# Half of one gate ahead of the mixing projection, and the transposes of the first tiles one product step later

## The chip, the cores and the metric

The kernel runs on one core of one Trainium2 chip. The metric is the time of one execution on the device in microseconds (us): the median of several runs. One more execution was recorded by the hardware profiler, and the rows shown below are from it. The engines are called as in the profile: PE (TensorE, matrix products and transposes), PEld (its weight loads), DVE (VectorE), ACT (ScalarE), POOL (GpSimd) and SP (SyncE, which issues most of the loads). Each engine, and each DMA queue, works its instructions off in the order in which they were laid down.

## The reference

One layer of an encoder with d = 1024 and 1024 tokens, all in float32:

```
x = x + 1/2 * post1(SwiGLU_1(pre1(x)))          # FFN 1, inner width 2816
u = pre_mix(x)
ret_q, ret_k, ret_v, ret_g, na_q, na_k, na_v, gate_ret, gate_na = split(u @ W_mix_in)
y_ret = (silu(ret_g) * headnorm(retention in both directions)) @ W_ret_out
y_na  = (neighbourhood attention on a 16 x 64 grid, with bias) @ W_na_out
x = x + post_mix((sigmoid(gate_ret) * y_ret + sigmoid(gate_na) * y_na) @ W_mix_out)
x = x + 1/2 * post2(SwiGLU_2(pre2(x)))          # FFN 2
```

pre, post and headnorm are RMS norms. `gate_na` is a 1024 x 1024 array: eight blocks of 128 channels, each for two halves of 512 tokens. The change is about the first half of its block 4.

## The kernel before

Every float32 operand is split into two parts, h (a cast on ACT) and l (a subtraction on DVE, `split`, lines 60 and 61), and each product is the sum of three matmuls (`mm3`, lines 87 to 89): h with h, h with l, l with h. Weights come by `load_w`: a 512 KB load on SP's queue into one of three `wraw` buffers, then two pieces of 512 columns, each one cast on ACT and one subtraction on DVE (`wl`, line 61), in a ring of eight pieces. There are eight PSUM banks: six of tag `ps`, two of tag `pt`.

The large products use seven half-size products instead of eight (Winograd's form). Tokens are handled in eight tiles of 128, t0 to t7. For such a product the left operand needs, beside its quarters a11, a12 (tiles t0 to t3) and a22, four sums s1 to s4, which are made while the tiles t4 to t7 are put away (`Winograd.put`).

The stages in order, with their place in the profile: FFN 1 in; FFN 1 out (`ffn_out`, up to about 681 us); the last tiles of it (to about 738 us); the mixing projection (`Pairs.run` over `jobs`, to about 1030 us); neighbourhood attention (`na_cores`); retention (`ret_cores`, to about 1449 us); its output product and W_mix_out; FFN 2 in; FFN 2 out.

**FFN out.** `ffn_out` walks 77 steps, n = 11 i + k: seven products i, eleven steps k of 12 matmuls each. Products with even i use four `ps` banks, those with odd i use two `ps` and two `pt`. After the fifth product (i = 4) the rows of t0 to t3 are complete. What is left for each, the four stages of `stages`, is put in the list `later`, and one entry is taken off ahead of the matmuls of each of the following steps, from n = 55 on:

- stage 0: a sum of squares finished on DVE (line 488) and its power -1/2 on POOL (`rstd`, line 97)
- stage 1: two residual additions on DVE (line 493), two stores of x on SP's queue, two squares on ACT (line 496)
- stage 2: the second norm's sum (DVE, line 500), `rstd` on POOL, two scalings on DVE (line 504)
- stage 3: eight transposes on PE (`flip`, line 126) into `ps` banks while i = 5 and into `pt` banks after it, and `put`: casts on ACT, subtractions on DVE.

So t0 has the steps 55 to 58, t1 59 to 62, t2 63 to 66, t3 67 to 70. At the end of the sixth product (i = 5, n = 65) `p2` adds to the four banks (DVE, line 581), and a square on ACT (line 482) reads the result and uses the bank as its waste, the `pt` banks too. In FFN 2 out there is no second norm: `stages` has the first two entries only.

**Between FFN out and the mixing projection.** `ffn_out` returns four `flips`, those of t4 to t7. Each makes its first four transposes into a `pt` bank, whose put copies to ACT (line 272) and forms part of s3 on DVE (lines 276, 277), and its second four into another, whose put splits a22 and makes s1, s2 and s3 (DVE 282, 284 and three subtractions; POOL 287, 288 for s4). Between them PE is given other work by a `Filler`: a generator of steps of three matmuls, of which so many are taken as the tuple `FLIP_FILL` says:

```
    fill = Filler(first())
    for f, k in zip(rest, FLIP_FILL):
        fill(k)
        f = f()
        if f is not None:
            fill(FLIP_FILL[4])
            f()
```

`first()` gives 32 steps of `vproj` (na_v for t0 to t3; line 1120 copies its banks out) and 24 of `mx.leads()`, the first products of the three first jobs, which fill all six `ps` banks. What is left is drained, and then the first job's `run` copies its lead to SBUF (line 376) and starts on the product with s2.

**The attention stages.** `products()` is the second filler: 385 steps in all: ret_v (128 steps and a mark), the blocks 4 to 7 of `gate_na` (`gate`, 16 steps each, sigmoid on ACT, line 1210), `gate_ret`, and the product W_na_out (64 steps, multiplied with the gate on DVE, line 1243). `NA_FILL` takes 12 + 34 x 4 = 148 steps in neighbourhood attention and `RET_FILL` takes 14 + 4 x 54 + 4 = 234 in retention. The last three are drained behind it. The last retention chunks go through `norm` (lines 929 to 937, with `rstd` on POOL), transposes (line 946), and a multiplication (line 947) with a tile `rg` that is loaded on SP's queue into one of two buffers. The product W_ret_out then starts on `xy`, the split of what retention has stored.

The order on each engine is not the text's order alone: a planner puts the instructions of each engine in a list by its own estimates of when they are ready, with the text's order as priority. An instruction whose operands it holds to be ready may be placed before an earlier one.

Of the kernel before, what the change touches and what calls it, by code (L numbers as in the profile page):

```python
# [10 lines left out]
F32 = mybir.dt.float32  # L11
F32R = mybir.dt.float32r
AF = mybir.ActivationFunctionType
# [5 lines left out]
P = 128  # L19
D = 1024  # L20
S = 1024
KT = D // P
# [6 lines left out]

NA_FILL = (12, 2, 2)  # L30
RET_FILL = (14, 2, 2, 4, 2, 3, 0, 1, 2)
FLIP_FILL = (8, 8, 8, 8, 2)
NA_UNITS = ((0, 0, 0), (3, 1, 0), (1, 0, 1), (1, 0, 2), (4, 1, 1), (4, 1, 2), (2, 0, 3), (5, 1, 3))
KEY_OFF = (0, 8, 24, 32)
RET_SCALE = 128 ** -0.5
# [387 lines left out]
class LeftFactors:  # L423


    order = [j + h * FT // 2 for j in range(FT // 2) for h in range(2)]
# [108 lines left out]
def ffn_out(c, q, blocks, junk, xtile, w_out, t_out, gl, ep, side={}):  # L535


    nc = c.nc
    NK = FT // 2
    tt = nc.vector.tensor_tensor  # L540
    later, rest, flips, xs = [], [], [], {}

    def xload(t):

# [23 lines left out]
    def p4(u, b):  # L568
        tt(q[3][:, u], b, q[3][:, u], ALU.add)
        ep.square(u, 0, q[3][:, u], b)  # L570
        later.extend(stages(u, (q[3][:, u], q[2][:, u])))

    def stages(t, halves):
        g = ep.steps(t, xs[t], halves)

        f = []
        return [lambda: next(g), lambda: next(g)] + [
            lambda: f.append(next(g)), lambda: f[0](*(("ps", 6) if i < 6 else ("pt", 2)))] * (ep.pre is not None)
# [431 lines left out]
def trunk_layer(ctx: ExitStack, tc, x, g1a, w1i, w1o, g1b, gma, wmt, wnv, wrv, logits, dtab, rope, bias,  # L1010
                wro, wno, wmo, gmb, g2a, w2i, w2o, g2b, out):
    nc = tc.nc
# [5 lines left out]
    c = Core(tc, const, wpool, psum, dram)  # L1018
# [4 lines left out]
    def dt(name, shape):  # L1023
        return dram.tile(shape, F32, name=name)
# [4 lines left out]
    d = {  # L1029
        "a21": dt("a21", [P, 4, 512]),  # L1030
        "nq": dt("nq", [NHP, P, S]), "nk": dt("nk", [NHP, P, S]), "nv": dt("nv", [16, 64, 512]), "nvg": dt("nvg", [4, 4, P, 512]),
        "no": dt("no", [NHP, P, S]), "rq": dt("rq", [RH, P, S]), "rk": dt("rk", [RH, P, S]),
        "rv": dt("rv", [TT, P, D]), "rg": dt("rg", [8, P, S]), "ry": dt("ry", [8, P, S]),
        "sr": dt("sr", [8, P, S]), "sn": dt("sn", [8, P, S]), "z": dt("z", [8, P, S]), "m": dt("m", [8, P, S]),
    }
# [24 lines left out]
    with (tc.tile_pool(name="tw1", bufs=1, reuse_waits="tile") as tw,  # L1060
# [12 lines left out]
    q = [ep.tile([P, 4, 512], F32, tag="q", name="q", bufs=2) for _ in range(2)]  # L1073
# [9 lines left out]
    rest = ffn_out(c, q, Blocks(c, (g0, g0, g0, g1), (3, 1)), junk,  # L1083
                   lambda t: (m1, m2, ep, ep)[t // 2].tile([P, D], F32, tag="xs", name="xs", bufs=2 + t // 4 * 2),
                   w1o, t1o, gl[0], fo,
                   {n: (lambda j=j: ahead.update({j: c.load_w(wnv[j])})) for j, n in enumerate((65, 66))})
# [8 lines left out]
    def xh(t, k):  # L1095

        return a21 if (t, k) == (1, 0) else wx.op(("a11", "a12", None, "a22")[2 * t + k])

    def vproj(src, groups, done):

        for toks in groups:
            banks = {t: c.bank() for t in toks}
            for k in range(KT):
                if k % 2 == 0:
                    w = ahead.pop(k // 2) if k // 2 in ahead else c.load_w(src[k // 2])
                for t in toks:
                    tt = slice((t % 4) * P, (t % 4 + 1) * P)
                    c.mm3(banks[t], [q[:, k % 4, tt] for q in xh(t // 4, k // 4)], w[k % 2], k == 0, k == KT - 1)
                    yield
            for t in toks:  # L1110
                done(t, banks[t])

    evpool = []

    def ev():
        return evpool[0].tile([P, S], F32, tag="ev", name="ev", bufs=3)
# [18 lines left out]
    jobs += [(32 + 2 * i, 33 + 2 * i, d["sn"][2 * i], d["sn"][2 * i + 1], AF.Sigmoid) for i in range(2)]  # L1135
    mx = Pairs(c, wx, [(wmt[j[0]], wmt[j[1]]) for j in jobs], 3)

    def first():
        yield from vproj(wnv, ((0, 1, 2, 3),), done_nv)
        yield from mx.leads()  # L1140

    fill = Filler(first())
    evpool[:] = [wx.tmp, None]
# [6 lines that stand above are left out]
    g_stack.close()  # L1150
    ep_stack.close()
    with tc.tile_pool(name="pa", bufs=1, reuse_waits="tile") as pa:
# [12 lines left out]
        for i, (_, _, f, g, fn) in enumerate(jobs):  # L1165
# [6 lines left out]
            def done(j):  # L1172
                h = j % 2
                if fn == "rotary":
                    rotate(turners[j], half(), parts[j], *tabs[h])
                elif fn is not None:
                    nc.scalar.activation(parts[j], parts[j], fn)
                c.store((f, g)[j // 2][:, h * 512:(h + 1) * 512], parts[j])
# [17 lines left out]
    mix.tile([P, 40], F32, name="pad")  # L1196
    evpool[:] = [mix]

    def gate(i, dst, halves=(0, 1)):

        w = c.load_w(wmt[i])
        e = ev()
        for h in halves:
            hs = slice(h * 512, (h + 1) * 512)
            b = c.bank()
            for k in range(KT):
                ks = slice((k % 4) * P, (k % 4 + 1) * P)
                c.mm3(b, [p[:, ks] for p in w[k // 4]], [q[:, k % 4] for q in xh(h, k // 4)], k == 0, k == KT - 1)
                yield
            nc.scalar.activation(e[:, hs], b, AF.Sigmoid)  # L1210
        hs = slice(halves[0] * 512, halves[-1] * 512 + 512)
        c.store(dst[:, hs], e[:, hs])

    def products():
        for j in range(2):
            yield from vproj(wrv[j], ((0, 1, 2), (3, 4, 5), (6, 7)), done_rv(j))
        yield "rv"
        for i in range(4, 8):
            yield from gate(32 + i, d["sn"][i])
        for i in range(4):  # L1220
            yield from gate(24 + i, d["sr"][i])
        for i in range(4, 8):
            yield from gate(24 + i, d["sr"][i], (1,))
        x1_stack.close()
        opool = pool(o_stack, "o", "right")
        oop = [opool.tile([P, 4, S], F32R, name=f"o{q}") for q in "hl"]
        for i in range(4, 8):
            raw = c.raw(d["no"][i - 4])
            c.split(oop[0][:, i - 4], oop[1][:, i - 4], raw)
            yield from gate(24 + i, d["sr"][i], (0,))  # L1230

        for i in range(8):
            if i % 2 == 0:
                w = c.load_w(wno[i // 2])
            e = ev()
            nc.sync.dma_start(e, d["sn"][i])
            for h in range(2):
                hs = slice(h * 512, (h + 1) * 512)
                b = c.bank()
                for k in range(4):  # L1240
                    c.mm3(b, [p[:, k * P:(k + 1) * P] for p in w[i % 2]], [q[:, k, hs] for q in oop], k == 0, k == 3)
                    yield
                nc.vector.tensor_tensor(e[:, hs], b, e[:, hs], ALU.mult)
            c.store(d["z"][i], e)
# [23 lines left out]
    for i0 in (0, 3, 6):  # L1268
        tiles = range(i0, min(i0 + 3, 8))
        m, z, w, banks = {}, {}, {}, {}  # L1270
# [16 lines left out]
        for i in tiles:  # L1287
            for k in range(KT if i0 > 0 else 0):
                one(i, k)
            for h in range(2):  # L1290
                hs = slice(h * 512, (h + 1) * 512)
# [11 lines left out]
    with tc.tile_pool(name="ep2", bufs=1, reuse_waits="tile") as ep:  # L1303
        rest = c.out_proj(KT, stream(c, gs, lambda k: d["m"][k]), lambda k: c.load_w(wmo[k]),
                          Ep(c, ep, gmb, g2a, False, rows(x1), rows(x2), wx.put))
# [19 lines left out]
    q = [op.tile([P, 4, 512], F32, tag="q", name="q", bufs=4) for _ in range(4)]  # L1325
# [86 lines left out]
```

## Time and profile before

| | before |
|---|---|
| median of 3 runs | 2304.51 us (2303.83 to 2305.05) |
| profiled execution, its own time | 2306.69 us |
| span in its trace, first to last instruction | 2304.8 us |
| PE busy | 2218.8 us, 96% |
| DVE busy | 1675.8 us, 73% |
| ACT busy | 1003.4 us, 44% |
| POOL busy | 593.1 us, 26% |
| mean granted clock of TensorE | 0.989 |

The profiled execution took 2.2 us longer than the median of the runs, and 1.9 us of its time lie outside its span. Shares of the span are averages over stages with different limits, so the stages have to be read one by one. In a row of the timeline the first number is the start in us from the span's start, the second how long the row lasted; xN says that N instructions of one kind are merged in it; the brackets hold the idle time of the engine just before it, and what ended it. Matmul rows overlap: what a matmul takes of PE is the distance between two starts.

### The profile page before, as it was taken

To read this page: it belongs to the slowest core of one execution; us is meant where nothing else is said; L and a number is where in the kernel's file an instruction comes from. 1 tells how busy PE (TensorE), PEld (TensorE's weight loads), DVE (VectorE), ACT (ScalarE), POOL (GpSimd) and SP (SyncE) were. 2 spreads that over 40 slices of the span, in tenths; PEclk is the share of its full clock that TensorE was granted. 3 is DMA by queue.
4 is the path that set the end of the run, shared out by engine and by line. 5 is a ranking of instruction groups with operands and counts; after the bars stand their busy time and mean duration, and the time that the engine had idled before them with its cause. 6 is when DMAs were issued, how large, how long until landed. Compare 5 with 4: busy or idle time off the path is not lost.

```text
span 2304.8 us, 30361 instructions
## 1 busy us (share of the span) xinstructions
PE 2218.8 (96%) x10288; PEld 1839.6 (80%) x10288; DVE 1675.8 (73%) x2945; ACT 1003.4 (44%) x2102; POOL 593.1 (26%) x689
## 2 busy tenths in 40 slices
PE   6999999999998999999999999999799999998998
PEld 5788888778776877778888888887588888887886
DVE  7897777645778758869875688547897777774576
ACT  6333332244554322258885675225533322233453
POOL 5342423210124134411101222101534242421012
PEclk9999999999999999999999999999899999999999
DMA  5464545477654542257645577866555454546765
GB/s 177 153 205 147 178 144 176 153 231 227 207 192 142 178 165 96 110 185 238 220 161 178 163 222 235 291 213 204 173 172 187 151 173 146 174 138 213 233 199 185
DMA packets 163675, 422.63 MB, mean 183 GB/s; under 512 B 19712, under 2 KB 47488, under 8 KB 163456
## 3 DMA queue, kind: packets, MB, share of 16 engines
q1 hardware_dynamic: 130080, 310.04, 42.4%
q0 software_dynamic: 33440, 110.65, 12.4%
q8 instruction: 81, 1.33, 0.2%
q14 instruction: 74, 0.61, 0.1%
HBM read 301.60 MB, written 123.21 MB: 184 GB/s over the span
## 4 chain that ended last, share of the span: by engine, by line
PE 80%; DVE 11%; issue 3%; POOL 3%; DMA 1%; ACT 1%; SPq 0%; POOLq 0%; DVEq 0%; ACTq 0%
PE ps L89 25%; PE ps L87 24%; PE ps L88 24%; DVE wl L61 2%; PE pt L89 1%; PE pt L87 1%; PE pt L88 1%; POOL rstd L97 1%; PE ps L725 1%; PE pt L744 1%; POOL cmb L287 1%; DVE tmp L117 1%; DVE t L378 1%; POOL cmb L288 1%; DVE xs L493 1%
## 5 line engine op out<-in xcount | busy, mean ns | idle before, releaser
L61 DVE TENSOR_TENSOR wl<-wraw,wh 128x512 fp32r<-128x512 f32 x662 | 468.9, 728 | 80.4 <-ACT wh L60 79.4
L60 ACT CAST wh<-wraw 128x512 fp32r<-128x512 f32 x670 | 390.3, 618 | 218.2 <-PE ps L88 71.2
L87 PE MATMUL ps<-wh,gh 128*128 128x512 f32 x612 | 241.5, 396 | 19.2 <-ACT gh L60 18.1
L61 DVE TENSOR_TENSOR gl<-graw,gh 128x512 fp32r<-128x512 f32 (+2 forms) x178 | 124.3, 699 | 173.8 <-ACT gh L60 173.6
L88 PE MATMUL ps<-wl,gh 128*128 128x512 f32 x612 | 241.2, 395 | 2.1 <-DVE wl L61 2.1
L89 PE MATMUL ps<-wh,gl 128*128 128x512 f32 x612 | 240.1, 395 | 0.8 <-DVE gl L61 0.5
L60 ACT CAST gh<-graw 128x512 fp32r<-128x512 f32 (+2 forms) x178 | 107.1, 602 | 226.6 <-PE ps L88 87.4
L414 ACT ACTIVATE c<-c 128x512 f32<-128x512 f32 x88 | 55.7, 633 | 283.1 <-DVE c L384 198.5
L87 PEld LDWEIGHTS ps<-wh,gh 128*128 128x128 f32 x612 | 116.4, 190 | 45.9 <-ACT gh L60 19.7
L89 PEld LDWEIGHTS ps<-wh,gl 128*128 128x128 f32 x612 | 116.4, 191 | 28.2 <-DVE gl L61 4.0
L88 PEld LDWEIGHTS ps<-wl,gh 128*128 128x128 f32 x612 | 116.6, 191 | 26.8 <-DVE wl L61 3.2
L483 POOL TENSOR_TENSOR q<-q,gain 128x512 f32<-128x512 f32 x22 | 33.6, 1546 | 357.7 <-ACT ps L482 343.4
L60 ACT CAST wh<-t 128x512 fp32r<-128x512 f32 x58 | 36.1, 622 | 202.6 <-DVE t L378 184.5
L89 PE MATMUL ps<-a12h,wl 128*128 128x512 f32 x280 | 110.4, 394 | 3.7 <-DVE wl L61 3.7
L87 PE MATMUL ps<-a11h,wh 128*128 128x512 f32 x280 | 112.4, 401 | 1.4 <-ACT wh L60 0.7
L89 PE MATMUL ps<-a11h,wl 128*128 128x512 f32 x280 | 110.9, 396 | 0.7 <-DVE wl L61 0.7
L87 PE MATMUL ps<-a12h,wh 128*128 128x512 f32 x280 | 111.1, 397 | 0.0
L88 PE MATMUL ps<-a11l,wh 128*128 128x512 f32 x280 | 111.0, 397 | 0.0
L88 PE MATMUL ps<-a12l,wh 128*128 128x512 f32 x280 | 109.8, 392 | 0.0
L87 PE MATMUL ps<-a22h,wh 128*128 128x512 f32 x280 | 109.8, 392 | 0.0
L89 PE MATMUL ps<-a22h,wl 128*128 128x512 f32 x280 | 109.1, 390 | 0.0
L88 PE MATMUL ps<-a22l,wh 128*128 128x512 f32 x280 | 109.0, 389 | 0.0
(354 smaller groups left out, 5975.6 us busy)
## 6 DMA issues: line engine op xcount, KB each, us to landing
wraw<-in_dram SPq DMA_DIRECT2D x243, 512.0 KB, 4.4
tw<-in_dram SPq DMA_DIRECT2D x88, 256.0 KB, 3.3
t<-tw POOLq DMA_DIRECT2D x88, 256.0 KB, 4.2
wraw<-t SPq DMA_DIRECT2D x40, 512.0 KB, 3.6
g0s<-cmb POOLq DMA_DIRECT2D x44, 256.0 KB, 4.2
graw<-g0s SPq DMA_DIRECT2D x44, 256.0 KB, 2.8
g1s<-cmb POOLq DMA_DIRECT2D x44, 256.0 KB, 4.2
graw<-g1s SPq DMA_DIRECT2D x44, 256.0 KB, 2.7
```

The costliest lines, as they stand in the source:

```text
L60: nc.scalar.copy(h, src)
L61: (eng or nc.vector).tensor_tensor(l, src, hf, ALU.subtract)
L87: mm(ps, a[0], b[0], start=start, stop=False)
L88: mm(ps, a[0], b[1], start=False, stop=False)
L89: mm(ps, a[1], b[0], start=False, stop=stop)
L97: self.nc.gpsimd.tensor_tensor(r[:, :n], ms, self.mhalf[:, :n], ALU.pow)
L117: nc.vector.scalar_tensor_tensor(xn[:, bs], x[:, bs], r[:, 0:1], gain[:, bs], op0=ALU.mult, op1=ALU.mult)
L287: nc.gpsimd.tensor_tensor(s3, h2, s3, ALU.subtract)
L288: nc.gpsimd.tensor_tensor(s3, s3, l2, ALU.add)
L378: tt(t2, b22, t1, ALU.subtract)
L414: nc.scalar.activation(gate[j], gate[j], AF.Silu)
L483: (eng or c.nc.gpsimd).tensor_tensor(h if out is None else out, h, self.post[:, b * 512:(b + 1) * 512], ALU.mult)
```

## The change

It has two parts.

In `ffn_out` the stages of the four tiles are gathered in `chains` and put into `later` in a merged order. With four stages each, the order becomes t0: 0, 1, 2; t1: 0; t0: 3; t1: 1, 2; t2: 0; t1: 3; and so on. The transposes of t0, t1 and t2 go to the steps 59, 63 and 67, one later than before, stage 0 of t1, t2 and t3 goes to 58, 62 and 66, one earlier, and all other stages keep their step, the transposes of t3 (70) too. With two stages each, in FFN 2 out, stage 1 of t0, t1 and t2 and stage 0 of the next tile change places.

The first half (tokens 0 to 511) of block 4 of `gate_na`, eight steps of three matmuls, is taken out of `products()` and put between `vproj` and `mx.leads()`. The second half stays where it was, so that this block's weights are loaded and split twice, and its result is stored in two halves. `FLIP_FILL` takes two steps more ahead of the transposes of t5, t6 and t7 each. `NA_FILL` and `RET_FILL` are as before; `products()` has 377 steps.

```
-FLIP_FILL = (8, 8, 8, 8, 2)
+EARLY = 4
+FLIP_FILL = (8, 10, 10, 10, 2)
...
-    later, rest, flips, xs = [], [], [], {}
+    later, rest, flips, xs, chains = [], [], [], {}, []
...
     def p4(u, b):
         tt(q[3][:, u], b, q[3][:, u], ALU.add)
         ep.square(u, 0, q[3][:, u], b)
-        later.extend(stages(u, (q[3][:, u], q[2][:, u])))
+        chains.append(stages(u, (q[3][:, u], q[2][:, u])))
+        if u == 3:
+            n = len(chains[0])
+            order = sorted((n * t + j + (j == n - 1) - .5 * (j == 0 and t > 0), t, j) for t in range(4) for j in range(n))
+            later.extend(chains[t][j] for _, t, j in order)
...
+    def gate(i, dst, halves=(0, 1)):
+
+        w = c.load_w(wmt[i])
+        n = len(halves) * 512
+        e = ev() if len(evpool) == 1 else evpool[0].tile([P, 512], F32, tag="ev", name="ev", bufs=4)
+        for j, h in enumerate(halves):
+            b = c.bank()
+            for k in range(KT):
+                ks = slice((k % 4) * P, (k % 4 + 1) * P)
+                c.mm3(b, [p[:, ks] for p in w[k // 4]], [q[:, k % 4] for q in xh(h, k // 4)], k == 0, k == KT - 1)
+                yield
+            nc.scalar.activation(e[:, j * 512:(j + 1) * 512], b, AF.Sigmoid)
+        c.store(dst[:, halves[0] * 512:halves[0] * 512 + n], e[:, :n])
+
     def first():
         yield from vproj(wnv, ((0, 1, 2, 3),), done_nv)
+        yield from gate(32 + EARLY, d["sn"][EARLY], (0,))
         yield from mx.leads()
...
         for i in range(4, 8):
-            yield from gate(32 + i, d["sn"][i])
+            yield from gate(32 + i, d["sn"][i], (1,) if i == EARLY else (0, 1))
```

More of the change, by code (lines that the diff above doesn't have):

```diff
@@ L1197, in trunk_layer @@
     evpool[:] = [mix]
[L1199 to L1212, printed above, removed]
     def products():
```

## Prediction

> **What bounds the kernel now.** I read the page first, then PE's waits around the change, then the busy times by stage, and then the timeline of each queue in the stages where PE waits.
>
> ```profile
> PE 2218.8 (96%) x10288; PEld 1839.6 (80%) x10288; DVE 1675.8 (73%) x2945; ACT 1003.4 (44%) x2102; POOL 593.1 (26%) x689
> ...
> PE 80%; DVE 11%; issue 3%; POOL 3%; DMA 1%; ACT 1%; SPq 0%; POOLq 0%; DVEq 0%; ACTq 0%
> ```
> PE bounds the whole: it is busy 96% of the span and holds 80% of the chain that ended last. A gain must come from PE's idle places. Those near the change, from 600 to 760 us:
>
> ```profile
> PE pt L126 <- ACT cmb L272: 3.4, 1, 3.4
> PE pt L126 <- DVE cmb L284: 3.4, 2, 2.4
> PE ps L126 <- DVE q L504: 2.3, 1, 2.3
> PE pt L126 <- ACT pt L482: 1.9, 1, 1.9
> ```
> The third and fourth row are transposes of t0 and t2 inside FFN out (4.2 us together); the first two, 6.8 us, are transposes of t5 to t7 behind it. The change aims at both pairs. What runs dry there is seen by stage (columns: length, then busy us of PE, PEld, DVE, ACT, POOL, then clock, DMA share, GB/s):
>
> ```profile
> 615.00:653.00 38.00, 35.70 (x166) 29.29 (x165) 32.86 (x55) 22.91 (x52) 11.10 (x12) 1.00 0.75 255
> 653.00:681.00 28.00, 26.14 (x123) 21.43 (x122) 19.04 (x28) 14.25 (x30) 7.31 (x5) 1.00 0.53 160
> 681.00:738.00 57.00, 49.60 (x225) 40.17 (x224) 52.84 (x76) 30.53 (x64) 30.87 (x31) 0.97 0.38 130
> 1400.00:1443.00 43.00, 43.00 (x254) 37.89 (x253) 34.87 (x91) 23.12 (x66) 10.69 (x18) 1.00 0.69 228
> ...
> 641.60:653.10 11.50, 11.50 (x53) 9.54 (x52) 10.77 (x18) 6.71 (x15) 1.02 (x2) 1.00 0.75 242
> ```
> From 681 to 738 us DVE is busy 52.84 of 57 us, more than PE: the tiles' chain, not PE, sets the end there. From 615 to 653 DVE has 32.86 of 38 and PE 35.70. In retention (fourth row) PE has no idle at all. The last row is the stretch just before line 581 (part 1).
>
> **Part 1, transposes a step later.** One step is 12 matmuls; starts are 0.227 us apart (652.53 and 654.12 below enclose eight), so 2.72 us. Three tiles' transposes with their casts and subtractions go back by that, three stages 0 (DVE 488, POOL 97) come forward by one, nothing on SP's queue changes place.
>
> ```profile
> 628.70 1.29 PE L126 MATMUL ps<-ident,q 128*128 128x128 f32 x8 [2.27 <-DVE q L504]
> ...
> 652.53 0.39 PE L87 MATMUL ps<-wh,gh 128*128 128x512 f32 x1
> ...
> 653.13 1.28 DVE L581 TENSOR_TENSOR q<-ps,q 128x512 f32<-128x512 f32 x2
> ...
> 654.12 0.39 PE L88 MATMUL ps<-wl,gh 128*128 128x512 f32 x1
> ...
> 655.60 0.59 ACT L482 ACTIVATE pt<-q 128x512 f32<-128x512 f32 x1
> ...
> 656.37 1.27 PE L126 MATMUL pt<-ident,q 128*128 128x128 f32 x8 [1.86 <-ACT pt L482]
> ```
> The wait of t0 (2.27 us) closes: 12 matmuls, 2.72 us, now run in it. But what opens the `pt` banks for t2 is DVE's line 581, and DVE did not wait for PE before it: from 641.6 us to 653.1 us it was busy 10.77 of 11.50 us (last row by stage). If DVE keeps its time, the banks open near 656.37 as before, and PE, 2.27 us early, waits there about 3.5 us. It then has only done four matmuls more than before (12 in place of the eight above): 4 x 0.227 = 0.9 us. Bounds: both waits gone, 2.27 + 1.86 = 4.1 us saved; below, nothing saved. I take -0.9, because the DVE rows are the nearest. What is late next is line 581 itself. In FFN 2 out no transposes hang on the list, and stage 1 and 0 change places beside a PE that does not wait: nothing; without that cover, one DVE row of 0.75.
>
> **Part 2, the half gate behind FFN out.** It adds 24 matmuls to PE there, 24 x 0.227 = 5.4 us, which the 6.8 us of waits above can hold. It also adds one 512 KB load on SP's queue, two casts on ACT, two subtractions on DVE, a sigmoid, and one store on POOL's queue. What they meet:
>
> ```profile
> 709.73 1.61 POOL L288 TENSOR_TENSOR cmb<-cmb,a12l 128x512 f32<-128x512 f32 x1
> 710.12 1.77 DVE L61 TENSOR_TENSOR wl<-wraw,wh 128x512 fp32r<-128x512 f32 x1
> ...
> 713.82 0.68 DVE L61 TENSOR_TENSOR wl<-wraw,wh 128x512 fp32r<-128x512 f32 x1
> ...
> 722.83 0.62 ACT L60 CAST s2h<-cmb 128x512 fp32r<-128x512 f32 x1 [2.42 <-DVE cmb L284]
> ...
> 724.24 0.72 POOL L67 DMA_DIRECT2D a<-cmb  x1 [2.71 <-ACT cmb L272]
> ...
> 733.02 0.61 DVE s2l L61
> ...
> 733.70 1.68 POOL cmb L287
> ...
> 737.10 0.62 ACT s4h L60
> 737.72 0.49 ACT ev L376
> ...
> 738.26 0.50 PE ps L87
> ...
> L1210 ACT ACT_TABLE_LOAD x2 | 2.6, 1283 | 0.0
> ...
> L1210 ACT ACTIVATE ev<-ps 128x512 f32<-128x512 f32 x24 | 14.2, 592 | 6.0 <-PE ps L89 5.9
> ```
> The rows from 733.02 to 738.26 are the end of the chain: t7's s2 on DVE, s4 on POOL, its cast on ACT, behind which in ACT's queue stands the copy that gives the bank back, and then PE. Whatever lands ahead of 733.02 in DVE's queue moves this end. Two `wl` at 0.68 are 1.4 us; at 1.77, beside a POOL operation, 3.5 us; placed into DVE's waits before 700 us, nothing. I take +1.4, most `wl` of the stage being like the row at 713.82. The casts fit ACT's gaps (2.42 us ahead of 722.83). The sigmoid brings a table load, 1.28 + 0.59 = 1.9 us, since Silu was the last function; it would come near that same gap, and I count nothing, with 1.9 as its bound if the gap is gone. Silu then needs its table again in the projection, where ACT has room: nothing. The load on SP stands between others that are two or three buffers ahead, the store (0.72 at most) fits POOL's 2.71 us gap: nothing each, and 0.7 for the store without it. The 5.4 us of matmuls end before the chain does.
>
> The Trainium skill, SBUF — State Buffer, section "Who interferes with whom", says that a DVE instruction with two operands in SBUF and a GpSimd operation that reads SBUF exclude each other for a whole instruction. The row of 1.77 us beside a POOL row agrees. By the page alone, with both pieces blocked, this part would cost an estimated 3.5 us, which is the upper bound above.
>
> **Part 3, eight steps fewer for attention.** The second filler loses the same 24 matmuls, and while PE is full (fourth row by stage) that should be 5.4 us. But the calls ask for 382 of then 377 steps, where there were 385. All fills up to the last chunk's matmuls get what they got; missing are the steps behind them: 3, 2 and the 3 drained ones, eight in all, between 1443.16 and 1449.21.
>
> ```profile
> 1442.91 0.28 PE L89 MATMUL ps<-sfh,ql 128*128 128x256 f32 x1
> ...
> 1445.77 0.51 ACT L937 ACTIVATE yn<-y,rstd 128x256 f32<-128x256 f32 x1 [0.94 <-POOL rstd L97]
> ...
> 1447.18 0.42 DVE L947 TENSOR_TENSOR rg<-pt,rg 128x256 f32<-128x256 f32 x1 [2.10 <-DMA rg<-rg]
> 1447.53 0.68 DVE L1243 TENSOR_TENSOR ev<-ps,ev 128x512 f32<-128x512 f32 x1
> ...
> 1448.12 1.22 DVE L61 TENSOR_TENSOR xy<-wraw,xy 128x1024 fp32r<-128x1024 f32 x1
> ...
> 1449.21 0.62 PE L87 MATMUL ps<-xy,wh 128*128 128x512 f32 x2
> ```
> They covered the norm of the last chunk: from PE's end (1442.91 + 0.28) to 1445.77 + 0.51 = 1446.28 its transposes can't start, and W_ret_out needs `xy`, whose subtraction at 1448.12 stands in DVE's queue behind a wait for a load (1447.18) that the fill does not move, and behind line 1243, which does go. So PE starts W_ret_out 1448.12 - 1447.53 = 0.6 us earlier, and not 5.4. Bounds: 0, and 1.9 us (`xy` as soon as its cast, begun behind 1446.28 and 1.0 long, is done); further if the planner brings W_ret_out forward. I take -0.6.
>
> **Sum.** -0.9 + 1.4 - 0.6 = -0.1 us: the profiled execution's 2306.69 becomes 2306.6, and the median of the runs, 2.18 below it, 2304.4. By the bounds of the parts this case lies between 2301.5 and 2307.5. A change of 0.2%, 4.6 us, is about what can be told from none.
>
> **Rivals.** (a) *The waits really close.* If DVE's lag in FFN out shrinks with the stages 0 that come early, 4.1 us are gained there; the two `wl` go into DVE's waits (0), and the tail gives 1.9 us or, with W_ret_out brought forward, some 3: -6.0 to -7.1, a time near 2298. For it: both waits are the very ones that PE shows. Against: DVE's 0.7 us of idle in the 11.5 before line 581.
>
> (b) *Slower: the in-order queues of the last tiles.* The place is between 722.83 and 737.10. If both `wl` (3.5), the table load with the sigmoid (1.9) and the store (0.7) land ahead of the s2 and s4 of t6 and t7, that chain ends 6.1 us later; with -1.5 from the other parts, +4.6: 2309.1. It decides as soon as the sigmoid stands ahead of s2h in ACT's queue without a gap. For it: no slack behind 701 us on DVE. Against: 2.42 us gap on ACT.
>
> (c) *The clock.* PE's granted clock falls after some waits:
>
> ```profile
> 702.00:705.00 3.00, 0.41 (x4) 0.42 (x5) 3.00 (x6) 1.57 (x3) 0.17 (x1) 1.00 0.00 0
> ...
> 723.00:727.00 4.00, 4.00 (x13) 3.23 (x14) 4.00 (x7) 1.43 (x3) 2.68 (x3) 0.57 0.57 151
> ```
> After 2.39 us of wait the clock was 0.57 for 4 us, (1 - 0.57) x 4 = 1.7 us lost; in a wait of 3.42 us it stayed at 1.00. There it costs nothing, the chain being longer. At the end of retention a new wait of some 5 us, broken only by transposes, stands ahead of a PE-bound stage: +1.7, so 2306.1; a second such loss at t2's longer wait makes 2307.8. The Trainium skill, TensorE: Matmul & The Clock Gate, Part 1, says that one idle window of about 3.4 us halves the clock and one busy window restores it, the windows running freely; the two rows agree in kind. By it the tail would lose an estimated 1.7 us, the amount above.
>
> **Chances.** Forecast 0.42; (a) 0.22; (b) 0.14; (c) 0.22. (c) stays within 4.6 us, so same has 0.42 + 0.22 = 0.64, faster 0.22, slower 0.14. The range reaches from (a) to (b), 2298.5 to 2309.
>
> **What would show it.** Right: t0's transposes without a wait, those of t2 behind one of over 2 us; s2 of the first job at the same distance from the end of FFN out or 1 to 3 us more; a PE wait of over 2 us ahead of the last transposes of line 946. Wrong: line 581 earlier with PE (then a), PE full through the end of retention, or the chain's end moved by 5 us (b).

## The result and the profile after

| | before | after |
|---|---|---|
| median of the runs | 2304.17 us | 2316.48 us (2313.48 to 2318.50) |
| profiled execution, its span | 2304.8 us | 2314.2 us |
| mean granted clock of TensorE | 0.989 | 0.986 |

The change makes the kernel slower: ratio 1.0045, 95% interval 1.0033 to 1.0057, some 10 to 12 us (by the interval, 8 to 13). In the profile's list of busy times PE has grown by 6.2 us over the 2218.8 of before, with as many instructions, so the matmuls themselves ran slower somewhere:

```profile
PE 2225.0 (96%) x10288; PEld 1844.8 (80%) x10288; DVE 1678.6 (73%) x2947; ACT 1005.1 (43%) x2104; POOL 592.2 (26%) x690
```

Line numbers of the changed kernel are one higher than before up to line 570, and five higher behind it (126 becomes 127, 482 483, 581 586, 937 942, 946 951); in `put`, 272 is 273, 276 to 288 are 277 to 289, and 376 is 377. The waits of PE from 600 to 760 us (releaser, total us, times, longest), in the place of the four rows of before:

```profile
PE ps L88 <- ACT ev L377: 3.8, 1, 3.8
PE pt L127 <- ACT pt L483: 3.6, 1, 3.6
PE pt L127 <- ACT cmb L273: 2.7, 1, 2.7
PE pt L127 <- DVE cmb L285: 1.1, 1, 1.1
```

t0's wait of 2.3 us is gone. t2's has grown from 1.9 to 3.6, the two waits behind FFN out have shrunk from 6.8 to 3.8 together, and ahead of the first job there is one of 3.8 where the kernel before had one of 0.8.

**FFN out.** The timeline of t0's transposes (first row) and around t2's:

```profile
630.16 1.03 PE L127 MATMUL ps<-ident,q 128*128 128x128 f32 x8
...
654.27 1.28 DVE L586 TENSOR_TENSOR q<-ps,q 128x512 f32<-128x512 f32 x2
...
657.36 0.58 ACT L483 ACTIVATE pt<-q 128x512 f32<-128x512 f32 x1
...
657.51 1.97 PE L127 MATMUL pt<-ident,q 128*128 128x128 f32 x8 [3.65 <-ACT pt L483]
```

The bank opens 1.1 us later than before, where the whole stage began 0.9 us later: DVE has not moved, and PE waits for it. What follows the wait is new. In the busy times by stretch (length, PE, PEld, DVE, ACT, POOL, clock, DMA share, GB/s):

```profile
659.00:669.20 10.20, 10.20 (x38) 8.29 (x37) 8.05 (x10) 3.87 (x8) 3.11 (x2) 0.78 0.64 202
...
689.00:746.00 57.00, 49.58 (x227) 40.53 (x225) 51.96 (x74) 31.04 (x61) 28.91 (x28) 0.96 0.41 136
...
746.00:751.00 5.00, 4.88 (x12) 3.81 (x12) 0.00 (x0) 0.06 (x1) 0.92 (x1) 0.50 0.86 297
...
1460.00:1470.00 10.00, 10.00 (x41) 8.15 (x41) 5.21 (x6) 3.79 (x4) 0.73 (x1) 0.89 0.90 336
```

Behind t2's wait the clock is 0.78 over 10.20 us: (1 - 0.78) x 10.2 = 2.2 us lost. The eight transposes themselves take 1.97 us instead of 1.27, another 0.7. FFN out ends 2.88 us later than before, 1.94 of it made inside the stage.

**Behind FFN out.** From the last matmul of FFN out to the first with s2 (start to start) it is 57.0 us instead of 52.0. The second row of the windows has DVE at 51.96 of 57 us, as full as before. The timeline of the last two tiles:

```profile
717.33 1.03 PE L127 MATMUL pt<-ident,q 128*128 128x128 f32 x8
...
727.27 0.68 DVE L285 TENSOR_TENSOR cmb<-pt,cmb 128x512 f32<-128x512 f32 x1
727.51 0.60 ACT L1154 ACTIVATE ev<-ps 128x512 f32<-128x512 f32 x1
...
728.00 0.61 ACT L61 CAST s2h<-cmb 128x512 fp32r<-128x512 f32 x1
728.09 0.63 PE L127 MATMUL pt<-ident,q 128*128 128x128 f32 x4 [1.11 <-DVE cmb L285]
...
729.90 0.62 ACT L61 CAST wh<-t 128x512 fp32r<-128x512 f32 x1 [1.29 <-DVE t L379]
...
731.03 0.58 ACT L273 COPY cmb<-pt 128x512 f32<-128x512 f32 x1
...
733.30 1.77 DVE L277 TENSOR_TENSOR cmb<-a11h,cmb 128x512 f32<-128x512 f32 x1
...
741.57 1.70 POOL L288 TENSOR_TENSOR cmb<-a12h,cmb 128x512 f32<-128x512 f32 x1 [5.01 <-DVE s2l L62]
...
744.96 0.62 ACT L61 CAST s4h<-cmb 128x512 fp32r<-128x512 f32 x1 [3.02 <-POOL cmb L289]
745.49 0.58 ACT L377 COPY ev<-ps 128x512 f32<-128x512 f32 x1
...
746.12 0.80 PE L88 MATMUL ps<-s2h,wh 128*128 128x512 f32 x1 [3.77 <-ACT ev L377]
```

The kernel before at t7's last transposes, its copy and its first sum:

```profile
722.95 0.63 PE L126 MATMUL pt<-ident,q 128*128 128x128 f32 x4 [2.39 <-DVE cmb L284]
...
723.36 0.58 ACT L272 COPY cmb<-pt 128x512 f32<-128x512 f32 x1
...
724.52 0.68 DVE L276 TENSOR_TENSOR cmb<-a11h,cmb 128x512 f32<-128x512 f32 x1
```

The sigmoid's table load is over and it starts at 727.51, and the operand of t6's s2h becomes ready only at 727.95 (727.27 + 0.68): the sigmoid holds s2h up by next to nothing. The tiles' own chain is late: t6's transposes stand at 717.33 and t7's last at 728.09, where before's last were at 722.95. Of these 5.14 us, 2.88 come from FFN out and 2.26 are made here. Another 2.72 us are lost between those transposes and the first job: on DVE the first job's weight sums (lines 378, 379 and 387, from 728.47 us) and two `wl` now stand ahead of t7's first sum (line 277, at 733.30 instead of 724.52), and on ACT a cast that waits for one of these sums stands ahead of t7's copy (731.03 instead of 723.36). In the kernel before all three sums came behind t7's first. From there the same chain (s2l, POOL 288, s4h, the copy) runs to the first job, which starts 7.86 us later than before, and its first twelve matmuls run at clock 0.50 (last but one row of the windows), 2.5 us more.

**Retention.** Between attention's first matmul and the last retention product 2.3 us more are lost, with as many matmuls in that stretch (the 24 that are missing stood behind it). Up to about 1335 us the changed kernel is 1.9 us ahead there, as the kernel before has a half clock at the start of attention (0.50 from 1034.05 to 1037.46 us) which the changed one has not; by 1385 us it has lost 4.2. Two new waits in the list of PE's waits from 1200 to 1470 us, where before had none:

```profile
PE pt L951 <- ACT yn L942: 2.8, 1, 2.8
PE ps L88 <- DVE y L936: 2.0, 1, 2.0
```

The second was not foreseen. Its rows in the timeline:

```profile
1367.38 0.62 ACT L61 CAST wh<-wraw 128x512 fp32r<-128x512 f32 x1 [1.52 <-DMA wraw<-in_dram]
1367.91 0.41 ACT L939 ACTIVATE yn<-y 128x256 f32<-128x256 f32 x1
...
1372.92 0.39 PE L88 MATMUL ps<-vh,ah 128*128 128x256 f32 x1 [1.99 <-DVE y L936]
...
1458.78 2.93 PE L88 MATMUL ps<-xy,wh 128*128 128x512 f32 x6 [0.49 <-ACT xy L61]
```

ACT's queue stands at casts of the filler's weights until a load lands, and the norm of retention (line 939) stands behind them. The DMA engines are nearly full there (share 0.97), and after PE's wait the clock is 0.58:

```profile
1355.00:1368.00 13.00, 13.00 (x75) 11.35 (x74) 10.60 (x22) 8.60 (x20) 0.56 (x1) 1.00 0.97 338
...
1372.90:1377.00 4.10, 4.08 (x16) 3.69 (x17) 2.70 (x9) 2.84 (x9) 0.56 (x1) 0.58 0.29 116
```

The like stretch of the kernel before, 8 us earlier, had a DMA share of 0.80:

```profile
1347.00:1360.00 13.00, 13.00 (x75) 11.31 (x73) 9.92 (x21) 10.46 (x22) 1.70 (x3) 1.00 0.80 255
```

At the end of retention (the last timeline row) W_ret_out starts 1.66 us earlier against the last retention product than before. Behind its first matmul the clock is low again (0.89 over 1460:1470, last row of the windows), and at the end of W_ret_out 1.7 us of that are gone: +9.57 has become +11.26.

### The profile page after: what moved, and what is told of

It reads as the page before. It is cut to its first block, busy times and chain, and to the rows that moved or that the text cites. A ratio compares the mean times of both kernels' runs of the same rounds, so it can differ in the third digit from the quotient of the medians.

```text
span 2314.2 us, 30361 instructions
## 1 busy us (share of the span) xinstructions
PE 2225.0 (96%) x10288; PEld 1844.8 (80%) x10288; DVE 1678.6 (73%) x2947; ACT 1005.1 (43%) x2104; POOL 592.2 (26%) x690
```

## The experiments

The table has, for each kernel's profiled execution, the start of five matmuls against before's (us): the last of FFN out, the first with s2 of the first job, the first of neighbourhood attention, the first of W_ret_out, the last of the kernel. The runs of one kernel lie 2 to 4 us to either side of their median, so a difference of 1 us between two profiles is told only where its rows show it. The ratio is to the kernel before on the same chip.

| kernel | FFN out | first job | attention | W_ret_out | end | median | ratio, 95% |
|---|---|---|---|---|---|---|---|
| after | +2.88 | +7.86 | +8.92 | +9.57 | +9.42 | 2316.48 | 1.0045 (1.0033 to 1.0057) |
| e1_part1 | +0.22 | +0.24 | +2.42 | +1.70 | +1.84 | 2308.33 | 1.0011 (1.0002 to 1.0020) |
| e2_part2 | -0.55 | +4.43 | +5.68 | +9.26 | +9.42 | 2316.53 | 1.0049 (1.0037 to 1.0062) |
| e3_half_gate_gone | -0.37 | -0.36 | -0.60 | -0.33 | +0.63 | 2308.52 | 1.0012 (1.0003 to 1.0021) |
| e4_ret6 | +1.53 | +6.53 | +7.64 | +3.88 | +4.00 | 2307.92 | 1.0010 (1.0001 to 1.0018) |
| f1_part2_ret6 | +0.88 | +6.04 | +6.39 | -0.74 | -1.29 | 2305.35 | 0.9998 (0.9989 to 1.0007) |
| f2_no_sigmoid | -0.58 | +5.83 | +8.50 | +3.54 | +2.66 | 2308.03 | 1.0009 (1.0000 to 1.0018) |
| f3_no_load | +0.85 | +4.72 | +6.96 | -0.59 | -1.40 | 2303.93 | 0.9993 (0.9984 to 1.0001) |
| f4_old_flipfill | +0.16 | +4.62 | +4.14 | -2.14 | -2.86 | 2301.86 | 0.9987 (0.9978 to 0.9996) |
| g1_mid | +0.55 | +6.55 | +8.09 | +3.17 | +2.66 | 2307.87 | 1.0009 (1.0000 to 1.0018) |
| g2_mid_late | -4.42 | +1.60 | +1.38 | -4.42 | -4.03 | 2302.64 | 0.9985 (0.9976 to 0.9994) |
| g3_late | -4.56 | -4.30 | -4.50 | -4.98 | -6.11 | 2301.73 | 0.9981 (0.9972 to 0.9990) |
| h1_late_f4 | -3.49 | -0.10 | -1.05 | -8.47 | -8.55 | 2298.72 | 0.9970 (0.9958 to 0.9982) |

**e1_part1: the kernel before with the merged order alone** (the `chains` lines of the diff).

> Only the first part: the transposes of t0 to t2 one step later, nothing of the gate. Theory A (a new wait of PE costs twice, by itself and by the half clock behind it): the wait of t0 closes, t2's transposes wait 3 to 4 us for the pt banks, which open no earlier, and about 4 us at half clock follow; the last matmul of FFN out comes 1 to 2.5 us later than before against the start of FFN out, and the execution is 1 to 2.5 us slower, 0.05 to 0.1%. Theory B (the loss is all from the gate's work behind FFN out; the first part is as forecast): 0.9 us faster, no half clock after t2's transposes. If both waits closed, 4 us faster.

Slower by 2.4 us in the medians (by the interval, 0.5 to 4.6). PE waits 4.0 us for t2's bank, and the half clock follows. In the timeline:

```profile
655.88 1.27 PE L126 MATMUL pt<-ident,q 128*128 128x128 f32 x8 [3.98 <-ACT pt L482]
...
657.81 0.63 PE L89 MATMUL ps<-wh,gl 128*128 128x512 f32 x1
658.23 0.63 PE L87 MATMUL ps<-wh,gh 128*128 128x512 f32 x1
```

Two starts are 0.42 us apart instead of 0.227. The stage ends 0.34 us later against its own start (-0.12), less than theory A's 1 to 2.5: the half clock (1.7 us) eats what the earlier transposes had won. The rest of this execution's loss stands behind the first job, whose wait of 2.4 us is followed by a half clock as well (+0.24 becomes +1.77 in its twelve matmuls with s2). In the kernel before the half clock fell earlier, at 723 us, where PE had time to spare. Where it falls differs from one execution to the next (last section), so that this second loss comes from the new order is not shown.

**e2_part2: the changed kernel with the old order of the stages.**

```
-            order = sorted(...)
-            later.extend(chains[t][j] for _, t, j in order)
+            later.extend(f for ch in chains for f in ch)
```

> Only the second part: half a gate and its fills between FFN out and the mixing projection, the stages of t0 to t3 in their old order. Theory A: from the last matmul of FFN out to the first s2 product of the projection 3 to 5 us more than before's 52.0, two half clocks there; in retention the 2 us wait at the chunk behind the halves of gate_ret comes again with its half clock, 4 us; the end of retention as in the changed kernel. In all 6 to 9 us slower. Theory B: the stretch behind FFN out takes the whole 8 to 10 us, and retention is as long as before.

As slow as the change: the half gate and the fills alone cost some 10 us, 5.0 of them between FFN out and the first job, and 3.6 between attention's start and W_ret_out (+5.68 to +9.26), where 24 matmuls fewer should have given something. Theory A's places held, though the wait in the middle of retention (1.8 us) had no half clock behind it this time; its sum, 6 to 9 us, was too low.

**e3_half_gate_gone: the kernel before without the first half of block 4.** `products()` asks for the second half only, and stores it twice in place of the first; 24 matmuls are left out.

> The kernel before, with the first half of block 4 of gate_na left out of the attention filler (the second half is stored in its place) and computed nowhere: 24 matmuls, 5.4 us of PE work, less, and every later step of the filler meets the attention chain eight steps earlier. Theory A (steps taken off a filler whose end is not refilled are worth nothing, and the shift brings a new wait): 0 to 4 us slower although it does less, with a PE wait of about 2 us in the first third of a head in retention and one of 2 to 3 us ahead of the last transposes. Forecast's own part 3: 0.6 us faster. If PE work alone counted: 5.4 us faster.

Nothing moves up to attention, and 24 matmuls less, 5.4 us of PE, make the kernel 2.6 us slower. Of the 5.4 us nothing arrives at W_ret_out (-0.60 at attention, -0.33 there): the fills take the same number of steps, so every later step of the filler meets another place in retention's loop, and the wait at the end opens. The half clock behind it takes 1.7 us more (W_ret_out ends at +1.40). Of the waits from 1200 to 1470 us the longest is:

```profile
PE pt L946 <- ACT yn L937: 2.5, 1, 2.5
```

The wait of 2 us in the middle of retention, which theory A expected too, did not come: PE waited there for `y` twice, 0.7 us in all. So the shift by eight steps brings the wait at the end by itself; what else the long one in the middle needs is open.

**e4_ret6: the changed kernel with eight steps less at the start of retention.**

```
-RET_FILL = (14, 2, 2, 4, 2, 3, 0, 1, 2)
+RET_FILL = (6, 2, 2, 4, 2, 3, 0, 1, 2)
```

> The changed kernel with 6 in place of 14 as the first number of the retention fills, so that from there on each part of retention meets the same filler steps as in the kernel before, the last eight of them too. Theory A: both new waits of retention go with their half clocks (4 us in the middle, 1.7 behind the end) and the 24 matmuls are really saved ahead of retention, 5.4 us: 7 to 11 us faster than the changed kernel, about the time of the kernel before. Theory B (loss all behind FFN out): 0 to 1 us faster than the changed kernel. If the first transposes of retention lack cover with 6 steps, a wait of 1 to 3 us shows there instead.

Now each later step of the filler meets retention where it did before. Both new waits of retention are gone (one of 2.1 us, with a half clock, has come early in attention, at 1064 us), and from attention to W_ret_out the kernel gains 3.8 us on before where the change lost 0.7; by the ratios 8 us come from one number. That the steps' places decide over retention's loss is shown by this pair; which load does it first is not.

**f1_part2_ret6, f2_no_sigmoid, f3_no_load: what of the half gate costs.** f1 is the kernel before with the half gate, the new `FLIP_FILL` and the short `RET_FILL`. f2 is f1 with a plain copy in place of the early sigmoid; f3 is f1 with the pieces of na_v's last weights in place of the half gate's own load, casts and subtractions.

```
f2: nc.scalar.activation(e[...], b, AF.Copy if len(evpool) > 1 else AF.Sigmoid)
f3: w = c.load_w(wmt[i]) if len(evpool) == 1 else spare
```

> The second part of the change with 6 as the first number of the retention fills, and the stages of t0 to t3 in their old order: the base of the three runs beside it. From the runs so far: retention as in the run with 6 fills, FFN out as before, so the time of the kernel before within 2 us; the stretch from the last matmul of FFN out to the first s2 product stays 57 us, 5 more than before's 52.0.

> As the base, but the early half of the gate is copied out without its sigmoid, so that no table is loaded there (the sigmoid of that half is left out). Theory S (the table load and the sigmoid stand ahead of t6's s2 on ACT and delay the chain of the last tiles): 1.3 to 1.9 us shorter behind FFN out. Theory D (DVE and PE set that chain; the operand of t6's s2 came only when the sigmoid ended): 0 to 0.5 us.

> As the base, but the early half gate uses the pieces of na_v's last weights, which are there already, in place of its own: one 512 KB load, two casts on ACT and two subtractions on DVE fewer (that half of the gate is computed with wrong weights). Theory D: DVE has no slack there, and each piece of 0.6 to 1.4 us moves the end: 1.2 to 3 us shorter. Theory P (the two extra steps ahead of each tile's transposes, that is PE's order, cost it): 0 to 0.5 us.

f1 equals before: what is lost behind FFN out comes back in attention and retention. From the last matmul of FFN out to the first with s2 it is 57.14 us in f1, 58.40 in f2 and 55.86 in f3. Leaving the sigmoid and its table load out gained nothing there: the planner ordered DVE and ACT otherwise without them, and it took 1.3 us more, so their own price is not separated. Without the load and its two `wl` the first job starts 1.3 us earlier, but nothing of that is left at its operand s1 (+7.18 in f3, +7.23 in f1), as f3 has 6.8 us of half clock there and f1 3.4. Some 4 of the 5 us are left to the matmuls, their places and the order on DVE that comes with them.

**f4_old_flipfill: f1 with the fills of before ahead of the transposes** (`FLIP_FILL = (8, 8, 8, 8, 2)`), so that eight steps more than in the kernel before (six more than in f1) are drained at the end.

> As the base, with 8 in place of 10 steps ahead of the transposes of t5, t6 and t7, as in the kernel before; the six steps run with the drained ones at the end. Theory P: t6 and t7 get their transposes 2 to 4 us earlier and DVE and POOL finish near where they did before; then PE's own longer drain (six steps, 4.1 us, more) sets the end: 0 to 2 us shorter in all. Theory D: the chain stays as long as in the base, and the stretch is as long or up to 1 us longer.

Faster than both kernels, by 0.13% against the one before. t5's to t7's transposes are back at their times, within 0.2 us, and PE never waits at the first job:

```profile
740.14 0.58 ACT L377 COPY ev<-ps 128x512 f32<-128x512 f32 x1
...
742.20 0.39 PE L88 MATMUL ps<-a12h,wh 128*128 128x512 f32 x1
742.88 0.39 PE L88 MATMUL ps<-s2h,wh 128*128 128x512 f32 x1
```

The copy that opens the bank ends at 740.72, and PE has its own drained steps until 742.88. The first job is as late as in f3, but with no wait and no half clock behind it: its twelve matmuls with s2 keep their time (+4.62 to +4.46 at the next but one operand, s1), where f1 loses 1.2 us (+6.04 to +7.23).

**g1_mid: f4 with fill steps between a tile's two sets of transposes**, `(0, 4, 1, 3)` of them, in the very waits of before.

> f4_old_flipfill with fill steps also between the first and the second four transposes of t5, t6 and t7 (4, 1 and 3 of them), where PE waits for the two pt banks. Theory A (only the place of the half gate's matmuls is wrong: steps ahead of a tile's transposes delay its chain, steps left for the end delay the drain, but PE's own waits in front of the second four are free): the waits of 3.4, 1.0 and 2.4 us hold most of the eight steps, the transposes keep their times within 0.5 us, the drain is eight steps (5.4 us) shorter, and s2 of the first job starts 1 to 2 us later than before instead of 4.6; the kernel takes 2 to 4 us less than f4_old_flipfill, 2298 to 2300 us on this scale. Rival E (the banks' casts and copies, not PE, end that stretch): the steps placed in the waits bring copies and sigmoids into ACT's queue ahead of the tiles' casts, t6's and t7's transposes come 2 us or more later, and nothing is gained, 2301 to 2304 us.

Theory A failed, and rival E held in kind, by another place than it named: some 5 us slower than f4 by the ratios, and slower than either had it. The tiles' chain grows again, now on DVE:

```profile
725.99 0.63 PE L131 MATMUL pt<-ident,q 128*128 128x128 f32 x4 [2.42 <-DVE cmb L289]
...
731.57 0.68 DVE L400 TENSOR_TENSOR wraw<-wraw,t 128x512 f32<-128x512 f32 x1
...
732.27 1.68 DVE L281 TENSOR_TENSOR cmb<-a11h,cmb 128x512 f32<-128x512 f32 x1
...
744.81 0.80 PE L90 MATMUL ps<-s2h,wh 128*128 128x512 f32 x1 [5.92 <-ACT ev L381]
```

t7's last transposes come 3.0 us later, and on DVE the sums of the first job's weights (to line 400) now stand ahead of t7's first sum (281, before's 276), as in the changed kernel. The drain ends early, and PE waits 5.92 us for the chain.

**g3_late and g2_mid_late: the transposes in FFN out later still.** The steps are t0 59, t1 63, t2 69 and t3 72; the other stages fill the steps between. g3 is the kernel before with this alone, g2 is g1 with it.

```
at = {59: (0, 3), 63: (1, 3), 69: (2, 3), 72: (3, 3)}
slots = iter((t, j) for t in range(4) for j in range(3))
for n in range(55, 73):
    t, j = at[n] if n in at else next(slots, (None, None))
    later.append(None if t is None else chains[t][j])
```

> The kernel before with only that later order of the stages in FFN out (the first part of the change, with t2 and t3 two steps later than in it); no half gate, no other fill. Theory A: the last product of FFN out starts its last matmul 3 to 4 us earlier than before and the kernel takes 2 to 4 us less than before, where e1_part1 took 2.4 us more. Rival F: PE waits elsewhere in the same stretch, and it is within 1.5 us of before. Rival G (the time won in FFN out is lost at its end, where t3's and t4's transposes now stand closer): the stretch from the end of FFN out to the first job becomes 2 to 4 us longer, and the sum is nothing.

> g1_mid with the transposes in FFN out later still: t0 at step 59, t1 at 63, t2 at 69 and t3 at 72, the other stages in the free steps between. Theory A (the pt banks open at a time that DVE sets, so t2 has to come two steps later): neither t0's nor t2's transposes wait, 4 us are saved in FFN out, the half clock behind a wait does not occur there, and the kernel takes 3 to 4 us less than g1_mid. Rival F (DVE is the bound of that stretch as a whole): line 581 comes as much earlier as PE does, but the matmuls behind it wait for gl, wl or q instead, FFN out ends within 1 us of its time before, and the times are equal within 1 us; t3's later put also pushes t4's stages, and up to 2 us are lost behind FFN out.

The first theory held in both: FFN out ends 4.6 and 4.4 us earlier, and the kernels are 4.6 us faster than before and 5.2 faster than g1. In g3's timeline (its line 590 is before's 581) nothing waits at t2:

```profile
652.56 1.28 DVE L590 TENSOR_TENSOR q<-ps,q 128x512 f32<-128x512 f32 x2
...
655.65 0.58 ACT L482 ACTIVATE pt<-q 128x512 f32<-128x512 f32 x1
...
657.40 1.03 PE L126 MATMUL pt<-ident,q 128*128 128x128 f32 x8
...
659.37 0.50 PE L88 MATMUL ps<-wl,gh 128*128 128x512 f32 x1 [0.70 <-DVE wl L61]
```

The bank is free at 656.23 (655.65 + 0.58), about as before, and t2 comes behind it. PE has done matmuls in the meantime. Of rival F 0.70 us is left, at `wl`.

**h1_late_f4: g2 without the steps between the transposes**, that is f4 with g3's order.

> g2_mid_late without the fill steps between a tile's transposes: that is f4_old_flipfill with the later order of g3_late in FFN out. Theory A (the parts act in separate places): the 4.5 us that g3_late gains in FFN out, the 4.6 that the half gate costs behind it (the drain), and what f4_old_flipfill gets back in attention (about 7 us in its trace) add up, s2 of the first job stands within 0.5 us of before, and the kernel takes 2297 to 2300 us, less than g3_late. Rival H (the gain of f4_old_flipfill in attention lies in how its steps fall against the loads there, and a shift of 4.5 us moves them again): attention gives back less than 3 us, and it takes 2301 to 2304 us, no less than g3_late.

2298.72 us, the fastest: ratio 0.9970, 6.8 us less than before on the same chip. The parts add up: -3.5 at the end of FFN out, -0.1 at the first job, -8.5 at W_ret_out. Of the last, 1.7 us are the half clock at the start of attention that the profile of before has and this one has not; the medians' 6.8 are the surer figure. So the half gate can be moved with a gain (f4 shows it without the later transposes), if its steps are drained at the end and the retention fill is shortened by as many. Against g3 alone the gain is not clear of the noise: the two intervals overlap.

## Why the prediction was wrong

It forecast 2304.4 us, and it is 2316.48, above its whole range. Its steps in turn:

**Part 1 (-0.9).** The mechanism was right. t0's wait closed, DVE's line kept its time, and t2's wait was 3.65 us against "about 3.5" (by its own terms, 1.86 + 2.27 - 0.9, it is 3.2). The term was mis-sized because the half clock behind that wait stood only among the rivals, at 1.7: in the changed kernel's profile it took 2.2 us, and 0.7 more in the transposes. e1 alone makes FFN out 0.34 us longer in its profile, and the kernel 2.4 us slower in the medians, instead of 0.9 faster. What should have been drawn from the same rows is in g3: two steps later still and there is neither a wait nor a half clock, and 4.6 us are gained.

**Part 2 (+1.4).** The two `wl` have about the size that was given to them (f3: 1.3 us at the first job's start), and f2 gives no sign that the sigmoid costs anything. The failed step is that the 24 matmuls cost nothing, as work "which the 6.8 us of waits above can hold", and that the two `wl` alone move the end. The steps were not put into the waits. They stood ahead of the transposes of t5 to t7, on whose results the chain hangs: t7's last transposes come 5.1 us late (728.09 against 722.95), 2.9 of which came from FFN out. Behind them DVE worked on the first job's weights before it took up t7, 2.7 us more; the rows show that order, and no run separates it. So the stretch grew by 5.0 us, and the half clock behind the wait of 3.77 us took 2.5 more. "The 5.4 us of matmuls end before the chain does" came true only because the chain had grown. With the steps at the end instead (f4) it does not: they show in PE's drain, 4.6 us. In the waits themselves (g1) they push t7 behind other work on DVE again.

**Part 3 (-0.6).** The failed step is "All fills up to the last chunk's matmuls get what they got". They get the same number of steps, but each step is the one eight later in the list. The loads of `gate_ret` met others of retention, at a DMA share of 0.97 against 0.80 of before in the like stretch, ACT stood at casts, and PE waited 1.99 us and ran 4.1 us at 0.58 behind it. The rows show this order; e3 shows that the shift alone does not bring the long wait. The tail went as forecast, better even (-1.66 to the start of W_ret_out), but the half clock took 1.7 back, as rival (c) had it. e4 and f1 show what the removed matmuls are worth if the steps stay in place: 3.8 and 7.1 us between attention and W_ret_out, on both sides of the 5.4 that the prediction named and set aside. Of f1's 7.1, 1.7 are the half clock at the start of attention that before's profile has and f1's has not.

**The range and the rivals.** The 2301.5 to 2307.5 us given for this case do not follow from the bounds of the parts, which add up to -6.0 and +3.5; the whole range was too low all the same. (a) was wrong for this order. (b) named the right stretch and almost its size (6.1 us there, 5.0 measured), but by the sigmoid, which held up nothing, so its condition would have missed it. (c) was right in kind at three places (behind t2, behind the first job's wait, at the tail), and too small: it counted two of them. No rival joined (b) with (c), and none had a loss in the middle of retention.

**The clock.** The Trainium skill, TensorE: Matmul & The Clock Gate, Part 1, says that the clock halves after an idle window of about 3.4 us. The 1.99 us wait at 1372.92 was followed by 0.58 over 4.10 us, so here a shorter wait was enough. In the 3.41 us up to the half clock, which began at 1373.42, PE was busy for 1.42 us: the window was not idle but less than half full (see the last section).

## What to carry to other kernels

A wait in the trace is filled only by work that is placed at the wait. Steps put ahead of the instruction that starts the next link of the chain delay that link, and the order on the other queues changes with it, so look there for what has moved ahead of the chain. An in-order filler that hands out fixed numbers of steps moves every later step when a few are taken out, so a stage hundreds of microseconds away must be counted too, and its fill shortened where the steps left. Read when the releaser is done, and move the waiting operation behind that time (g3), not by one convenient step. Reckon with a half clock of 3.4 us or more, 1.7 us of PE's time, behind every wait of about 2 us that stands ahead of a full PE, and do not take one profile's word for whether it comes.

## What the hardware showed that was not expected

The same wait is followed by a half clock in one execution and not in another. e2 and f1 have the same code in FFN out and the same wait of 1.9 us at t2. FFN out ends at -0.55 in e2 and, behind a half clock, at +0.88 in f1. The wait of 3.42 us in the kernel before had no loss behind it, and the one of 1.99 us in the changed kernel had.

The traces show why. Each stretch of half clock between 600 and 1500 us lasts 3.41 us or twice that, and within one execution all begin whole multiples of 3.41 us apart, as on a fixed grid. The grid lies elsewhere in each execution. What counts is how busy PE was in one window of that grid. The windows around the wait, first in f1, then in e2, then around the wait of 3.42 us in the kernel before:

```profile
653.65:657.07 3.42, 1.51 (x11) 1.20 (x11) 3.42 (x5) 3.42 (x11) 3.16 (x3) 1.00 0.45 93
657.07:660.48 3.41, 3.41 (x10) 2.63 (x9) 3.41 (x5) 1.73 (x4) 3.18 (x2) 0.50 0.71 228
```

```profile
654.27:657.68 3.41, 1.86 (x12) 1.53 (x13) 3.41 (x5) 3.41 (x10) 3.41 (x3) 1.00 0.35 80
657.68:661.09 3.41, 3.41 (x17) 2.83 (x16) 3.41 (x5) 1.82 (x4) 2.78 (x2) 1.00 0.76 239
```

```profile
699.54:702.95 3.41, 1.63 (x10) 1.01 (x8) 2.98 (x6) 0.00 (x0) 0.60 (x1) 1.00 0.19 77
702.95:706.37 3.42, 1.78 (x10) 1.57 (x11) 3.42 (x7) 2.22 (x4) 0.74 (x1) 1.00 0.32 46
```

In f1 the whole wait lies in one window, PE is busy for 1.51 us of it, and the next window has clock 0.50. In e2 and in the kernel before the wait lies across a border, PE is busy for 1.63 us or more in each window, and the clock stays at 1.00. Over the fourteen traces, between 600 and 1500 us, every one of the 35 full-clock windows with PE busy for less than 1.45 us was followed by half clock, and none of those with more than 1.58 us; of the seven between, three were. So by these traces a single wait under about 1.8 us cost no clock, and one between that and some 3.7 us did or did not by where it fell (an estimate from the upper bound: 3.41 - 1.58 = 1.83, and twice that, as a wait across a border is shared by two windows). What a half clock behind a wait costs lay between nothing, where PE had time to spare, and some 2.5 us.

POOL's sum of line 288 took 1.70 us in the changed kernel and 3.48 us at the same place in f4 and h1:

```profile
734.73 3.48 POOL L288 TENSOR_TENSOR cmb<-a12h,cmb 128x512 f32<-128x512 f32 x1 [4.24 <-DVE s2l L62]
```

(In h1 it is line 292, at 731.63.) In f4 DVE's two `wl` beside it took 1.28 us; in the kernel before, at the same place, the two took 3.47 us and POOL's sum 1.67. So it is the one or the other that takes longer when they meet; no run was made to tell what decides it, and the cause is open. POOL's longer sum makes up most of the 2.5 us by which f4's chain to the first job ended later than before's.
